# Masks of the maxima on GpSimd, maxima paced by an estimate, and an earlier start of the output weights in a hybrid S5 and attention step

## The chip, the cores and the metric

The kernel runs on one core of a Trainium2 chip. The metric is the device time of one execution in microseconds (us). The core has five engines that work side by side, each through its own queue: TensorE (PE: matrix products; PEld is its loading of weights), VectorE (DVE), ScalarE (ACT), GpSimd (POOL) and SyncE (SP), which here issues the DMA transfers. TensorE writes to banks of PSUM, and the on-chip memory for everything else is SBUF.

## The reference

One layer of an encoder is computed for a prompt of 2048 rows and for 64 further rows (the decode rows) with a cache of 512 earlier ones:

```python
mod = silu(c) @ w_ada + b_ada;  shift, scale, gate = split(mod)
proj = (rmsnorm(x) * (1 + scale) + shift) @ w_in
u, z_s, q, k, v, z_a, f_logit = split(proj)
y_ssm = gelu(s5(u)); y_ssm = y_ssm * sigmoid(y_ssm @ w_glu + b_glu) * silu(z_s)
s = q @ k.T * scale + cum_q - cum_k         # cum: running sum of log-sigmoid(f_logit)
s = where(pos_k <= pos_q, s, -inf)
y_att = softmax(s) @ v * silu(z_a)
y = x + gate * (concat(y_ssm, y_att) @ w_out)
```

There are 8 heads of 64 channels. The change touches the attention, from the scores to the softmax, and the loading of `w_out`. The softmax needs, for each query and head, the maximum of its scores; here it is found ahead of the scores themselves, by a cruder product.

## The kernel before

The program runs in stages: the modulation, the projection with the S5 part beside it (to about 742 us of the profile), the GLU of the S5 branch (to about 808), the attention (to about 1236) and the output projection (to the end).

**Tiles, blocks, units.** The heads go in four pairs, and a pair's two heads share the 128 partitions. For each pair there are five attention tiles, in the order of `self.order`: the decode rows (`qt` 4), then the prompt's queries in four tiles of 512 (`qt` 0 to 3). They are numbered 0 to 19, so 0, 5, 10 and 15 are decode tiles, and 4, 9, 14 and 19 are the longest. A tile's keys come in blocks of 128: 5 for a decode tile (four of the cache and one of the new rows) and 4, 8, 12 or 16 for the others. Two blocks make a unit of the loop in `run` (L1535). A unit computes the scores of its two blocks (`scores`, L1433: four passes for each head, then the exponential on ScalarE into a buffer `p`, then an addition of `p` to a running sum `acc`, on VectorE or POOL by turns), multiplies the unit before by the values (`mix`, L1480) and transposes one thing that was loaded (`turn`, L1343). The additions of `p` for a diagonal block after the first are narrower than 512 queries and all on VectorE.

**Loads.** `load` (L1279) is called twice a unit. It takes the next of `todo`, a tile of 512 keys or of 512 queries, when there are buffers for it. With the keys it also loads their forget bias `cb`, [128, 2, 512] in float32 and spread over all partitions, and holds it as long as the keys are used. There are six buffers for `cb` and three more from the start of the attention (L1514).

**Maxima.** A maximum (`maxima`, L1370) is one call for 128 queries of two heads against up to 512 keys: two matmuls into a twin bank, then two VectorE instructions that add the bias and take the maximum (L1398). Where the keys are those of the queries' own tile (the diagonal), or the new decode rows, four more matmuls add a mask `m_qk` through the identity `idb` (L1392 to L1394). Their order is the list `mx`: for each query tile, by 128 queries `t` and then by key tile. At most two are made for each of the 16 steps of the GLU (`MXU`, L1428) and two for each unit, one behind each block's scores (L1540), as long as there are any. When a tile's last is done, its maxima are transposed into `sm` by `turn`, and its scores can begin. There are 168 in all; 68 have a mask.

**Banks and order.** Scores and maxima share the twin banks in turn: two beside the GLU, three in the attention. TensorE's instructions keep the order in which the program writes them; the other queues are put in order by the planner at the time of building, which takes what is ready by its own reckoning.

**Output weights.** `Out.weights` (L1709) is a generator. Each step loads one block of `w_out`, 128x512, into one of three staging buffers `ost`, and for a block loaded two steps before it rounds the high part on ScalarE (`ohb`, L319) and subtracts on POOL to get the low part (`olb`, L205). It goes on only where SBUF is free. `run` begins with it when nothing is left of keys, queries and maxima (L1555) and then takes two steps a unit.

Of the kernel before, what the change touches and what calls it, by code (L numbers as in the profile page):

```python
# [17 lines left out]
P = 128  # L18
# [3 lines left out]
DEC = 64  # L22
# [20 lines left out]
PVG = 2  # L43
MXU = 2

# [144 lines left out]
def Step(tc, a, o, ctx):  # L190
# [76 lines left out]
    idb = [identb, cst.tile([P, P], BF16, name="identw")]  # L267
    m_qk, m_kq = ([cst.tile([P, P], BF16, name="%s%d" % (x, i)) for i in range(2)] for x in ("m_qk", "m_kq"))
    rj = cst.tile([P, P], F32, name="rj")
# [16 lines left out]
    def masks():  # L286
        tmp = Region(nc, R_S5W)
        swap = tmp.tile([P, P], F32, name="swap")
        PL.memset(swap, 0.0)
        for base in (64, -64):  # L290
            PL.affine_select(out=swap, in_=swap, compare_op=ALU.not_equal, fill=1.0, base=base,
                             pattern=[[-1, P]], channel_multiplier=1)
        V.tensor_copy(idb[1], swap)
        for sign, m in ((1, m_qk), (-1, m_kq)):
            for base in (0, 64, -64):
                x = tmp.tile([P, P], F32, name="msk")
                V.memset(x, 0.0)
                PL.affine_select(out=x, in_=x, compare_op=ALU.is_ge, fill=NEG, base=sign * base,
                                 pattern=[[-sign, P]], channel_multiplier=sign)
                r = slice(0, 64) if base == 64 else slice(64, P) if base else slice(0, P)  # L300
                V.tensor_copy(m[int(base != 0)][r], x[r])

# [867 lines left out]
class Attn:  # L1170
# [5 lines left out]
    def __init__(self, e):  # L1176
# [11 lines left out]
        self.cur = self.seen = self.unit = self.st = 0  # L1188
# [4 lines left out]
        self.todo, self.loaded, self.mx, self.smq = [], [], [], []  # L1193
        self.kv, self.values, self.q, self.ready = {}, {}, {}, {}
# [57 lines left out]
    def idle(self, tag):  # L1252

        now = self.seen if tag[0] == "c" else self.cur
        return sorted((x for x in self.held[tag] if x[2] < now), key=lambda x: x[2])
# [23 lines left out]
    def load(self):  # L1279
# [6 lines left out]
        if what == "k":  # L1286
            new = kind == "n"
            if not (self.can("kw" if new else "ks", 2) and self.can("cw" if new else "cb", 1)):
                return
# [11 lines left out]
            cb = self.claim([P, 2, w], "cw" if new else "cb", last, F32)  # L1301
            nc.sync.dma_start(cb, e.cb_d[2 * hp:2 * hp + 2, t0 * P:t0 * P + w].partition_broadcast(P))
            hi, lo = (self.claim([P, w], "kw" if new else "ks", last) for _ in range(2))
            self.kv[hp, kind] = hi, lo, cb, self.kb[:, t0 * P:], nt, rows, kind
        else:
# [37 lines left out]
    def turn(self):  # L1343
# [11 lines left out]
        elif self.loaded and self.loaded[0][0] + 2 <= self.unit:  # L1355
            _, (what, i, _), x, nt, rows, hi, lo = self.loaded.pop(0)
            pt = self.f.tile([P, 512], F32, tag="tr", name="tr")
            for t in range(nt):
                e.PE.transpose(pt[:, t * P:t * P + rows], x[:rows, t], e.ident[:rows, :rows])
            w = (nt - 1) * P + rows  # L1360
            e.S.copy(hi[:, :w], pt[:, :w])
            e.V.tensor_tensor(lo[:, :w], pt[:, :w], hi[:, :w], op=ALU.subtract)
            if what == "q":
                hp, qt = self.order[i]
                np = len(self.kinds(qt))
                for t in range(nt):
                    for pi in range(np):
                        self.mx.append((self.unit, i, t, pi, t == nt - 1 and pi == np - 1))

    def maxima(self):  # L1370

        e = self.e
        V, PE = e.V, e.PE
        if not self.mx or self.mx[0][0] >= self.unit:
            return
        _, i, t, pi, last = self.mx[0]
        hp, qt = self.order[i]
        if last and any(self.order[x[1]][0] == hp for x in self.smq):
            return
        self.mx.pop(0)  # L1380
        kinds = self.kinds(qt)
        nt = 4 if qt < 4 else 1
        if t == pi == 0:
            self.pm = self.mem.tile([P, 4, 2, 4], F32, tag="pm", name="pm")
        qh = self.q[i][0]
        kh, kl, cb, kb, kt, rows, kind = self.kv[hp, kinds[pi]]
# [3 lines left out]
        ops = [(ps[:, h, :n], qh[64 * h:64 * h + 64, ts], kh[64 * h:64 * h + 64, :n]) for h in range(2)]  # L1390
# [4 lines left out]
        self.pairs(ops, True, True)  # L1395
        for h in range(2):
            b = self.mem.tile([P, 512], BF16, tag="pb", name="pb")
            V.tensor_tensor_reduce(b[:, :n], ps[:, h, :n], cb[:, h, :n], 1.0, NEG, ALU.add, ALU.max,  # L1398
                                   accum_out=self.pm[:, t, h, pi:pi + 1])
        if last:  # L1400
            for h in range(2):
# [3 lines left out]
            self.seen = i + 1  # L1405

# [6 lines left out]
    def step(self):  # L1413
        self.unit += 1
        self.load()
        self.load()

    def glu(self, glu):
# [6 lines left out]
        for b in range(glu.steps):  # L1425
            self.step()
            glu.mm(b)
            for _ in range(MXU):  # L1428
                self.maxima()
            glu.part(b + 2)  # L1430
            self.turn()

    def scores(self, tile, kd, t):  # L1433

        e = self.e
        V, PL = e.V, e.PL
        kh, kl, cb, kb, kt, rows, kind = self.kv[tile.hp, kd]
        diag = kind == tile.qt or kind == "n"
# [54 lines left out]
    def sums(self, tile):  # L1493
# [12 lines left out]
        e.nc.sync.dma_start(e.ma_d[P * tile.hp:P * tile.hp + P, :, 64 * tile.qt:64 * tile.qt + n // TC], tile.z)  # L1506

    def run(self, out):

        e = self.e  # L1510
        self.f = Banks(e.psum, 0)
        for tag, kb, n in (("p", 4, 6), ("acc", 4, 4), ("z", 2, 2), ("w", 2, 2)):
            self.mem.ring(tag, int(1024 * kb), n)
        self.hold("cb", 4, 3)  # L1514
        weights = out.weights()
        pend = done = None
        self.forced = 0
        self.vload(0)
        for i, (hp, qt) in enumerate(self.order):
# [10 lines left out]
            e.nc.sync.dma_start(z, e.z_d[512 + P * hp:640 + P * hp, :, 64 * qt:64 * qt + nz // TC])  # L1530
            blocks = [(kd, t) for kd in self.kinds(qt) for t in range(self.kv[hp, kd][4])]
            tile = SimpleNamespace(hp=hp, qt=qt, nq=nq, nz=nz, z=z, q=self.q[i] + (self.ready[i],), acc=[None, None],
                                   given=[False, False], n=0, nb=len(blocks), po=None, rest=[],
                                   end=i >= len(self.order) - 2, last=i == len(self.order) - 1)
            for u in range(0, len(blocks), PVG):  # L1535
                self.step()
                group = []
                for kd, t in blocks[u:u + PVG]:
# [28 lines left out]
        out.mem.add(self.spare("vt"))  # L1567
        self.cur = self.seen = len(self.order)
        out.mem.add(self.spare("cb", "ks", "qs", "sm"))
        out.mem.join()  # L1570
# [84 lines left out]
class Out:  # L1655
# [12 lines left out]
    def __init__(self, e):  # L1668
# [4 lines left out]
        self.d, self.raw = [], []  # L1673
        self.near = self.cast = False
        self.ops = {}

# [32 lines left out]
    def weights(self):  # L1709
# [212 lines left out]
    def run(self, weights):  # L1922
# [14 lines left out]

        self.fetch("t3", 3, [self.mem.at("late", x, [P, 512], F32R) for x in self.mem.rings["ost"][2][1:]])
        for i, n in ((0, 1), (1, 1), (0, 0), (1, 0)):
# [195 lines left out]
```

## Time and profile before

| | us |
|---|---|
| median of 3 runs | 1406.46 (1403.91 to 1409.44) |
| span of the profiled execution, first to last instruction | 1410.9 |
| GLU | 742 to 808 |
| attention, 20 tiles | 812 to 1236 |
| last maximum starts | 1174.9 |
| first and last loads of output weights | 1107.2, 1222.6 |
| first and last subtractions of output weights | 1185.0, 1227.3 |
| span after the attention | 1236 to 1410.9 |

The profile comes from one execution and lists every instruction with its start, length, engine, line, and the tiles it writes and reads ("out<-in"). `twin` are banks of scores and maxima, `pb` and `pm` what a maximum writes, `p` the exponentials, `bank` other PSUM banks, `ohb`/`olb` the output weights. "Waits" name the engine and line that ended an idle time. A busy time of TensorE counts its instructions from start to modelled end; what a step costs is read from the starts of consecutive instructions.

### The profile page before, as it was taken

How to read it: one execution, taken by the hardware profiler on the slowest of the kernel's cores; microseconds unless marked ns; L12 is line 12 of the kernel's file. 1: busy time of each engine (PE TensorE's matmuls, PEld its weight loads, DVE VectorE, ACT ScalarE, POOL GpSimd, SP SyncE). 2: the span in 40 equal slices, each digit the busy share in tenths (PEclk: the TensorE clock that was granted, in tenths of full speed). 3: DMA queues.
4: the chain of work that ended last, by engine and by line, in shares of the span. 5: the costliest groups of instructions: out<-in, count | busy, mean ns of one | idle time of the engine just before them, and what ended most of it. 6: DMA issues, size and time to landing. Idle time of an engine off the chain costs nothing.

```text
span 1410.9 us, 25901 instructions
## 1 busy us (share of the span) xinstructions
PE 1318.9 (93%) x9164; PEld 1036.0 (73%) x9164; DVE 972.3 (69%) x2404; ACT 655.9 (46%) x1710; POOL 519.8 (37%) x502
## 2 busy tenths in 40 slices
PE   5898999999999899999899899999999999798998
PEld 2787999998888889898688755555555555387887
DVE  3635896987786679764326968786787786355775
ACT  3645365567443575574214435544544545522221
POOL 1100254566443446352004113423323325733453
PEclk9998999999999999999999979999999999999999
DMA  9894422534556835446239644124122123495542
GB/s 340 312 335 95 106 77 91 155 121 120 154 147 211 255 116 180 135 125 190 78 101 283 187 116 139 26 72 141 35 68 62 40 51 78 143 320 187 179 158 81
DMA packets 249476, 204.92 MB, mean 145 GB/s; under 512 B 91296, under 2 KB 217340, under 8 KB 248322
## 3 DMA queue, kind: packets, MB, share of 16 engines
q1 hardware_dynamic: 249346, 203.27, 47.0%
q8 instruction: 72, 1.18, 0.4%
q14 instruction: 58, 0.48, 0.1%
HBM read 137.68 MB, written 65.53 MB: 144 GB/s over the span
## 4 chain that ended last, share of the span: by engine, by line
PE 65%; DVE 13%; DMA 7%; issue 5%; ACT 3%; POOL 3%; SPq 3%; DVEq 0%; ACTq 0%; POOLq 0%
PE low L154 28%; PE twin L154 13%; PE bank L154 12%; PE last L154 7%; PE glu L154 2%; DMA wst<-in_w_in_dram 2%; DVE pb L1398 2%; PE bank L157 2%; DVE wlo L323 1%; POOL olb L205 1%; DMA x<-in_x_prompt_dram 1%; SPq L415 1%; PE low L157 1%; DMA lt<-t 1%; POOL qss L329 1%
## 5 line engine op out<-in xcount | busy, mean ns | idle before, releaser
L154 PE MATMUL low<-whi,h 128*128 128x256 f32 (+1 forms) x1584 | 294.6, 285 | 5.1 <-DVE th L608 4.0
L154 PE MATMUL low<-h,whi 128*128 128x256 f32 (+2 forms) x1152 | 277.3, 332 | 2.2 <-DVE th L608 1.4
L154 PEld LDWEIGHTS low<-whi,h 128*128 128x128 f32 x1584 | 248.1, 190 | 6.5 <-DVE th L608 4.2
L1398 DVE CUSTOM_DVE_ANT_0 pb<-twin,cb 128x512 bf16<-128x512 f32 (+3 forms) x328 | 200.0, 610 | 59.6 <-PE twin L154 49.8
L154 PE MATMUL low<-wlo,h 128*128 128x256 f32 (+1 forms) x816 | 229.7, 284 | 6.5 <-DVE wlo L323 6.5
L154 PEld LDWEIGHTS low<-h,whi 128*128 128x128 f32 x1152 | 197.3, 193 | 22.8 <-DVE h L323 1.9
L354 ACT ACTIVATE p<-twin 128x1024 f32<-128x1024 f32 (+3 forms) x180 | 149.8, 840 | 121.0 <-PE twin L154 110.7
L154 PE MATMUL low<-h,wlo 128*128 128x256 f32 (+2 forms) x576 | 189.4, 329 | 0.8 <-DVE wlo L323 0.8
L154 PEld LDWEIGHTS low<-wlo,h 128*128 128x128 f32 x816 | 154.8, 190 | 9.2 <-DVE wlo L323 8.8
L154 PE MATMUL bank<-p,vt 128*64 128x512 f32 (+3 forms) x704 | 143.2, 529 | 0.0
L154 PE MATMUL twin<-qs,ks 64*128 64x512 f32 (+3 forms) x1056 | 134.1, 359 | 0.0
L154 PEld LDWEIGHTS low<-h,wlo 128*128 128x128 f32 x576 | 111.4, 193 | 10.6 <-DVE wlo L323 1.9
L323 DVE TENSOR_TENSOR wlo<-wst,whi 128x512 fp32r<-128x512 f32 (+1 forms) x96 | 73.1, 767 | 66.4 <-ACT whi L319 66.1
L1476 DVE TENSOR_TENSOR acc<-acc,p 128x1024 f32<-128x1024 f32 (+4 forms) x88 | 90.1, 1024 | 30.0 <-ACT p L354 27.7
L329 POOL TENSOR_TENSOR qss<-qss,mhalf 128x4 f32<-128x4 f32 (+1 forms) x68 | 78.3, 1153 | 86.5 <-DVE qss L328 84.8
L154 PEld LDWEIGHTS twin<-qs,ks 64*128 64x128 f32 x1056 | 94.6, 190 | 11.0
L154 PE MATMUL twin<-sm,kb 64*128 64x512 f32 (+3 forms) x360 | 77.5, 426 | 22.2 <-DVE pm L1398 14.4
L154 PEld LDWEIGHTS bank<-p,vt 128*64 128x64 f32 x704 | 45.3, 140 | 64.5 <-issue 55.8
L319 ACT CAST whi<-wst 128x512 fp32r<-128x512 f32 (+1 forms) x96 | 58.8, 619 | 70.2 <-PE low L154 41.0
L205 POOL TENSOR_TENSOR x<-x,ot 128x512 f32<-128x512 f32 (+1 forms) x34 | 52.3, 1540 | 84.3 <-DVE ot L1803 79.3
L154 PEld LDWEIGHTS twin<-sm,kb 64*128 64x128 f32 x360 | 34.3, 186 | 63.0 <-DVE pm L1398 33.7
L645 ACT ACTIVATE hsq<-ev 128x64 bf16<-128x64 f32 (+1 forms) x272 | 69.8, 257 | 8.6
(437 smaller groups left out, 2641.6 us busy)
## 6 DMA issues: line engine op xcount, KB each, us to landing
wst<-in_w_in_dram SPq DMA_DIRECT2D x48, 512.0 KB
x<-in_x_prompt_dram SPq DMA_DIRECT2D x32, 512.0 KB
h<-h SPq DMA_DIRECT2D x16, 1024.0 KB
wada<-in_w_ada_dram SPq DMA_DIRECT2D x12, 1024.0 KB
cb<-cb_d SPq DMA_DIRECT2D x20, 512.0 KB
out_dram<-ev SPq DMA_DIRECT2D x64, 128.0 KB
out_dram<-x SPq DMA_DIRECT2D x32, 256.0 KB
z_d<-th SPq DMA_DIRECT2D x24, 256.0 KB
```

What stands on the lines that cost most here:

```text
L154: return self.keep(self.pe.matmul(*a, **kw))
L157: return self.keep(self.pe.transpose(*a, **kw))
L205: PL.tensor_tensor(out, x, y, op=op)
L319: i = S.copy(hi, x)
L323: V.tensor_tensor(lo, x, hi, op=ALU.subtract)
L329: PL.tensor_tensor(out, out, bc(mhalf[:out.shape[0]], list(out.shape)), op=ALU.pow)
L354: i = S.activation(out, x, func, **kw)
L415: x = nc.sync.dma_start(w[:, 4 * k2:4 * k2 + 4], e.w_ada[512 * k2:512 * k2 + 512, n * 512:n * 512 + 512] .rearrange("(k p) c -> p k c", p=P))
L645: S.activation(sq[:r], tv[:, h], AF.Square, accum_out=ss[:r, h:h + 1])
L1398: V.tensor_tensor_reduce(b[:, :n], ps[:, h, :n], cb[:, h, :n], 1.0, NEG, ALU.add, ALU.max, accum_out=self.pm[:, t, h, pi:pi + 1])
L1476: (PL if j else V).tensor_tensor(y[:rows, :, c0:nq], x[:rows, :, c0:nq], p[:rows, :, :n], op=ALU.add)
```

## The change

- **Masks.** `m_qk` becomes a float32 tile. The four mask matmuls go. Instead POOL adds the mask to the bias in place (`hide`): when the bias of a diagonal job is loaded, to its last 128 columns; after the maximum of 128 queries `t`, to the 128 columns before those, for the next one. So a job goes from `t` = 3 to 0.
- **Jobs and reloads.** The maxima are grouped in 48 jobs, one for each query tile and key tile. Each job loads its own bias into one of four buffers (`biases`, called once a unit), which comes free when the job is done. Before, the biases were loaded with the keys.
- **Pace.** `MXU` goes. `pace` keeps `lag`, an estimate of how far VectorE's work runs behind TensorE's: a unit adds VectorE's additions and takes off TensorE's time, a maximum adds the difference of its two shares. It makes up to two maxima while `lag` is below 2.3, and more only up to what is needed for the next tile to be ready (`left`); a second call after `turn` may make one more. Both calls stand behind the scores of both blocks.
- **Additions.** Narrower diagonal blocks now go to POOL by turns, too, once its running sum exists.
- **Output weights.** They begin when no keys and queries are left to load, one step a unit, and two once the maxima are done. There are four staging buffers, and a block is split three steps after its load. Once all maxima are done the subtraction is VectorE's. The SBUF that is given to them (`give`) includes what the smaller number of bias buffers leaves unused.

```diff
-MXU = 2
+GLU_PE, GLU_DVE, LAG = 3.7, 1.9, 2.3
...
-        for tag, kb, n in (("kw", 0.25, 4), ("vn", 0.5, 2), ("cw", 0.5, 2), ("cb", 4, 6), ("qs", 2, 12), ("sm", 2, 6),
+        for tag, kb, n in (("kw", 0.25, 4), ("vn", 0.5, 2), ("cw", 0.5, 2), ("cb", 4, 4), ("qs", 2, 12), ("sm", 2, 6),
...
+    def biases(self):
+        e = self.e
+        while len(self.bias_at) < len(self.jobs):
+            j = len(self.bias_at)
+            i, pi = self.jobs[j]
+            hp, qt = self.order[i]
+            kind = self.kinds(qt)[pi]
+            new = kind == "n"
+            if not self.can("cw" if new else "cb", 1):
+                return
+            w = DEC if new else 4 * P
+            t0 = 20 if new else 16 if kind == "c" else 4 * kind
+            cb = self.bias_at[j] = self.claim([P, 2, w], "cw" if new else "cb", j, F32)
+            e.nc.sync.dma_start(cb, e.cb_d[2 * hp:2 * hp + 2, t0 * P:t0 * P + w].partition_broadcast(P))
+            if new or kind == qt:
+                self.hide(cb, w)
+
+    def hide(self, cb, end):
+        w = min(end, P)
+        c = cb[:, :, end - w:end]
+        self.e.padd(c, c, self.e.m_qk[:, :w].unsqueeze(1).to_broadcast([P, 2, w]))
+
+    def left(self, i):
+        n = 0
+        for k, pi in self.jobs[self.job:]:
+            if k > i:
+                break
+            n += 4 if self.order[k][1] < 4 else 1
+        return n - self.place
...
+        t = nt - 1 - self.place
...
-        if kind == qt or kind == "n":
-            w = min(n, rows)
-            ops += [(ps[:, h, n - w:n], e.idb[m][64 * h:64 * h + 64], e.m_qk[m][64 * h:64 * h + 64, :w])
-                    for m in range(2) for h in range(2)]
...
+        if kind == qt and t:
+            self.hide(cb, t * P)
+        self.place += 1
...
+    def pace(self, pe, dve, least=0, most=2):
+        self.lag = max(0.0, self.lag + dve - pe)
+        done = 0
+        while done < most and (done < least or self.lag < LAG):
+            n = self.maxima()
+            if not n:
+                break
+            done += 1
+            self.lag += 2 * n / 960 + 0.25 - n / 2400
+        return done
...
-            for _ in range(MXU):
-                self.maxima()
+            self.pace(GLU_PE, GLU_DVE)
...
-        j = i % 2 if whole and not late else 0
+        j = i % 2 if not late and (whole or (acc[1] is not None and not tile.given[1])) else 0
+        if not j:
+            self.busy += 2 * n / 960 + 0.1
...
+    def give(self, out):
+        if not self.given:
+            self.given.append(None)
+            out.mem.add(self.ring("kn"))
+            out.mem.add([(a / 1024, b / 1024) for a, b in self.mem.segs if b > a])
+            self.mem.segs = []
+        out.mem.add(self.spare("ks", "qs"))
+        if len(self.bias_at) == len(self.jobs):
+            out.mem.add(self.spare("cb"))
+        if self.job == len(self.jobs) and not self.smq:
+            out.mem.add(self.spare("sm"))
...
-        self.hold("cb", 4, 3)
...
+        out.idle = lambda: self.job == len(self.jobs)
...
                 for kd, t in blocks[u:u + PVG]:
                     group.append(self.scores(tile, kd, t))
-                    self.maxima()
+                pe = 0.4 + sum(8.3 * x[4] for x in group) / 2400
+                units = (len(blocks) - u + PVG - 1) // PVG
+                need = self.left(i + 1)
+                need = -(-need // max(1, units - 1)) if need > 0 else 0
+                need -= self.pace(pe, self.busy, need)
...
-                if not (self.todo or self.loaded or self.mx or self.smq):
-                    if not self.given:
-                        out.mem.add(self.ring("kn"))
-                    out.mem.add(self.spare("cb", "ks", "qs", "sm"))
-                    next(weights, None)
+                self.pace(0.0, 0.0, need, 1)
+                if not (self.todo or self.loaded):
+                    self.give(out)
                     next(weights, None)
+                    if self.job == len(self.jobs):
+                        next(weights, None)
...
-        yield from wait(5)
-        mem.ring("ost", 2048, 3)
+        yield from wait(6)
+        mem.ring("ost", 2048, 4)
...
-            e.split(st, h, l, keep=True)
+            e.split(st, h, l, el=e.V if self.idle() else None, keep=True)
...
-                if len(late) == 2:
+                if len(late) == 3:
                     part()
```

More of the change, by code (lines that the diff above doesn't have):

```diff
@@ L267, in Step @@
     idb = [identb, cst.tile([P, P], BF16, name="identw")]
-    m_qk, m_kq = ([cst.tile([P, P], BF16, name="%s%d" % (x, i)) for i in range(2)] for x in ("m_qk", "m_kq"))
+    m_qk = cst.tile([P, P], F32, name="m_qk")
+    m_kq = [cst.tile([P, P], BF16, name="m_kq%d" % i) for i in range(2)]
     rj = cst.tile([P, P], F32, name="rj")
@@ L293, in masks @@
         V.tensor_copy(idb[1], swap)
[L294 to L301, printed above, removed]
+        V.memset(m_qk, 0.0)
+        PL.affine_select(out=m_qk, in_=m_qk, compare_op=ALU.is_ge, fill=NEG, base=0, pattern=[[-1, P]],
+                         channel_multiplier=1)
+        for base in (0, 64, -64):
+            x = tmp.tile([P, P], F32, name="msk")
+            V.memset(x, 0.0)
+            PL.affine_select(out=x, in_=x, compare_op=ALU.is_ge, fill=NEG, base=-base, pattern=[[1, P]],
+                             channel_multiplier=-1)
+            r = slice(0, 64) if base == 64 else slice(64, P) if base else slice(0, P)
+            V.tensor_copy(m_kq[int(base != 0)][r], x[r])
     mhalf = cst.tile([P, 1], F32, name="mhalf")
@@ L1287, in load @@
             new = kind == "n"
-            if not (self.can("kw" if new else "ks", 2) and self.can("cw" if new else "cb", 1)):
+            if not self.can("kw" if new else "ks", 2):
                 return
@@ L1363, in turn @@
             if what == "q":
[L1364 to L1368, printed above, removed]
+                self.qat[i] = self.unit
+    def biases(self):
[14 more added lines that the diff above has]
+                self.hide(cb, w)
@@ L1376, in maxima @@
-        _, i, t, pi, last = self.mx[0]
+        V = e.V
+        if self.job == len(self.jobs):
+            return 0
+        i, pi = self.jobs[self.job]
         hp, qt = self.order[i]
-        if last and any(self.order[x[1]][0] == hp for x in self.smq):
-            return
-        self.mx.pop(0)
         kinds = self.kinds(qt)
         nt = 4 if qt < 4 else 1
-        if t == pi == 0:
+        last = self.place == nt - 1
+        end = last and pi == len(kinds) - 1
+        if self.qat.get(i, self.unit) >= self.unit or self.job not in self.bias_at:
+            return 0
@@ L1384, in maxima @@
+        if end and any(self.order[x[1]][0] == hp for x in self.smq):
+            return 0
+        t = nt - 1 - self.place
+        if self.place == pi == 0:
             self.pm = self.mem.tile([P, 4, 2, 4], F32, tag="pm", name="pm")
         qh = self.q[i][0]
-        kh, kl, cb, kb, kt, rows, kind = self.kv[hp, kinds[pi]]
+        kh, kl, kb, kt, rows, kind = self.kv[hp, kinds[pi]]
+        cb = self.bias_at[self.job]
         ts = slice(t * P, t * P + P)
@@ L1399, in maxima @@
                                    accum_out=self.pm[:, t, h, pi:pi + 1])
+        if kind == qt and t:
+            self.hide(cb, t * P)
+        self.place += 1
         if last:
+            self.place = 0
+            self.job += 1
+        if end:
             for h in range(2):
@@ L1436, in scores @@
         V, PL = e.V, e.PL
-        kh, kl, cb, kb, kt, rows, kind = self.kv[tile.hp, kd]
+        kh, kl, kb, kt, rows, kind = self.kv[tile.hp, kd]
         diag = kind == tile.qt or kind == "n"
@@ L1567, in run @@
         out.mem.add(self.spare("vt"))
-        self.cur = self.seen = len(self.order)
-        out.mem.add(self.spare("cb", "ks", "qs", "sm"))
+        self.cur = len(self.order)
+        self.give(out)
         out.mem.join()
@@ L1674, in __init__ @@
         self.near = self.cast = False
+        self.idle = lambda: False
         self.ops = {}
@@ L1936, in run @@
         self.decode(0)
-        self.fetch("t3", 3, [self.mem.at("late", x, [P, 512], F32R) for x in self.mem.rings["ost"][2][1:]])
+        self.fetch("t3", 3, [self.mem.at("late", x, [P, 512], F32R) for x in self.mem.rings["ost"][2][:2]])
         for i, n in ((0, 1), (1, 1), (0, 0), (1, 0)):
```

26 lines of the change are left out of this document (13 added, 13 removed).

## The prediction

> **What bounds the kernel now.** I read the page first, then the windows by stage (cut where a tile of the attention begins), then who TensorE waits for in the stretches that are not full.
>
> ```profile
> span 1410.9 us, 25901 instructions
> ...
> PE 1318.9 (93%) x9164; PEld 1036.0 (73%) x9164; DVE 972.3 (69%) x2404; ACT 655.9 (46%) x1710; POOL 519.8 (37%) x502
> ```
>
> TensorE is the bound overall. The edits touch 742 to 1236 us. The columns are window, length, then busy time (instructions) of PE, PEld, DVE, ACT, POOL, the granted clock, DMA share, GB/s:
>
> ```profile
> core 0: us, PE busy (x) PEld busy (x) DVE busy (x) ACT busy (x) POOL busy (x), PEclk, DMA share, GB/s
> 742.00:812.00 70.00, 63.37 (x527) 57.58 (x527) 56.43 (x131) 31.46 (x61) 20.84 (x17) 0.99 0.80 239
> 812.00:835.00 23.00, 20.32 (x156) 13.14 (x154) 16.39 (x48) 6.28 (x14) 1.80 (x3) 0.65 0.54 157
> 835.00:922.00 87.00, 86.94 (x679) 46.86 (x675) 67.07 (x181) 43.49 (x54) 31.31 (x15) 1.00 0.27 73
> 922.00:940.00 18.00, 16.32 (x178) 10.70 (x178) 16.66 (x48) 7.50 (x15) 5.46 (x5) 1.00 0.29 75
> ...
> 1025.00:1044.00 19.00, 15.80 (x169) 9.91 (x169) 17.52 (x49) 7.13 (x15) 5.48 (x5) 1.00 0.22 56
> ...
> 1131.00:1150.00 19.00, 15.68 (x174) 9.92 (x174) 17.27 (x50) 6.92 (x14) 5.59 (x5) 1.00 0.27 47
> ...
> 1192.00:1236.00 44.00, 36.65 (x230) 17.21 (x230) 19.34 (x17) 23.27 (x34) 32.10 (x18) 0.92 0.53 147
> 1236.00:1411.00 175.00, 166.77 (x724) 136.51 (x720) 112.60 (x139) 35.61 (x62) 73.07 (x49) 0.97 0.54 185
> ```
>
> Long tiles (835 to 922) are TensorE's: 86.94 of 87, VectorE 77% busy. The three short stretches, where a head pair ends and two small tiles of the next begin, are VectorE's: 16.66 of 18, 17.52 of 19, 17.27 of 19. The last tile (1192 to 1236) is neither's: TensorE 36.65 of 44, POOL 32.10. TensorE's weight loads for the score banks wait there for the maxima (us, times, longest), in 811:835 and then the three short stretches:
>
> ```profile
> PEld twin L154 <- DVE pm L1398: 7.2, 4, 3.5
> ...
> PEld twin L154 <- DVE pm L1398: 3.1, 5, 1.2
> ...
> PEld twin L154 <- DVE pm L1398: 5.0, 7, 1.7
> ...
> PEld twin L154 <- DVE pm L1398: 5.1, 6, 1.5
> ```
>
> In the last tile it is a chain: a block of output weights waits for a free staging buffer, which POOL's subtraction gives back; ScalarE's rounding of that block waits for its landing; the exponentials stand behind the rounding.
>
> ```profile
> PE twin L154 <- ACT p L354: 7.3, 4, 2.3
> ...
> ACT ohb L319 <- DMA ost<-in_w_out_dram: 17.4, 7, 4.7
> ...
> SPq L1736 <- POOL olb L205: 22.6, 11, 4.2
> ...
> 1202.01 0.62 ACT L319 CAST ohb<-ost 128x512 fp32r<-128x512 f32 x1 [3.60 <-DMA ost<-in_w_out_dram]
> 1202.53 1.93 ACT L354 ACTIVATE p<-twin 128x1024 f32<-128x1024 f32 x2
> ...
> 1203.60 0.69 PE L154 MATMUL twin<-sm,kb 64*128 64x512 f32 x2 [2.33 <-ACT p L354]
> ```
>
> **The change, part by part.** Prices, mean ns behind the comma (the POOL rows with slashes give min/median/max):
>
> ```profile
> L1398 DVE CUSTOM_DVE_ANT_0 pb<-twin,cb 128x512 bf16<-128x512 f32 x232 | 159.5, 687 | 33.4 <-PE twin L154 27.0 <-DVE pm L1398 0.5 <-PE bank L154 0.3
> L1398 DVE DVE_READ_ACCUMULATOR2_ANT pm<- 128x1 f32 x336 | 27.8, 83 | 0.0
> ...
> L1476 DVE TENSOR_TENSOR acc<-acc,p 128x768 f32<-128x768 f32 x16 | 16.1, 1008 | 0.2
> ...
> L1362 DVE TENSOR_TENSOR ks<-bank,ks 128x512 fp32r<-128x512 f32 x20 | 13.8, 688 | 5.5 <-ACT ks L1361 5.5
> ...
> L1476 POOL TENSOR_TENSOR acc<-acc,p 128x1024 f32<-128x1024 f32 x22 | 52.3, 2379 | 44.1 <-ACT p L354 44.1
> ...
> L1476 POOL TENSOR_TENSOR acc<-p,p 128x256 f32<-128x256 f32 x4 | 2.9, 730 | 36.9 <-issue 26.4 <-ACT p L354 10.5
> ...
> L205 POOL TENSOR_TENSOR olb<-ost,ohb x16: 1264/1862/2264, 1185.0 to 1227.3; 128x512 fp32r<-128x512 f32 x16
> ```
>
> A full maximum (two heads, 512 keys) costs VectorE 2 x (0.687 + 0.083) = 1.54 us.
>
> *Output weights.* By the rules of the diff, counted unit by unit, the first block now starts in the last two units of tile 14 and ten of sixteen blocks are split, one a unit, before the last maximum; the other six go to VectorE (0.69 us each, the 688 row), which is busy 19.34 of 44 in the last tile. ScalarE's and POOL's shares move under tiles 14 to 18, where both have room (6.92 and 5.59 of 19): cost 0, or at most ten subtractions of 1.86 us = 19 us of POOL if its room is not where they fall. What goes is 7.3 us of TensorE's waits and, at clock 0.92, 0.08 x 44 = 3.5 us of slow clock. I take -10 of 10.8. Late next is TensorE itself. On SP the blocks now stand among the loads of values and gates of tiles 14 to 18, with one more staging buffer and a whole unit for each; one that waits there for POOL holds these loads up, which are a tile ahead: 0. The work after 1236 keeps its memory and its loads (the values' buffers still come free only then): 0.
>
> *Pacing.* Both versions make 20 maxima beside the GLU. Then tiles 0 and 1 get 4 instead of 9, and each of the three short stretches 5 instead of 9: 4 x 1.54 = 6.2 us less for VectorE in each, more than the 3.1, 5.0 and 5.1 us that TensorE waits. I take -11 of 13.2. In 811:835, of 7.2 us, 3.5 stand at the end of the GLU, where the last two maxima are as before or wider; the other 3.7 go: -4.
>
> ```profile
> 811.55 0.48 PE L154 MATMUL twin<-sm,kb 64*128 64x128 f32 x2 [3.22 <-DVE pm L1398]
> ...
> 810.00:815.00 5.00, 3.31 (x24) 2.73 (x25) 3.01 (x11) 0.98 (x3) 0.00 (x0) 0.62 1.07 291
> ...
> 820.00:825.00 5.00, 5.00 (x30) 3.08 (x30) 2.49 (x7) 0.97 (x2) 0.73 (x1) 0.51 0.70 207
> ```
>
> That stop is followed by half clock until 825, though TensorE is busy again from 811.55. [...]
>
> The removed maxima come back in the long tiles, up to three a unit: tiles 3 and 4 get 34 instead of 28. The estimate reckons 2 x 512/960 + 0.25 = 1.32 us for what the rows price at 1.54, and leaves out the key and query splits (0.69). For tiles 3 and 4 that is 6 x 1.54 = 9.2 us more on VectorE, less two diagonal pairs of adds (1.0 and about 0.5 us) that go to POOL: +6, where some 20 of 87 are idle, but in uneven lots. Its ends are 0, if the idle time takes it all, and three such pairs of tiles, 18; I take +5 over all of them, nearer the idle row.
>
> *Masks off TensorE.* Of 68 masked maxima, from the start of its score matmul to what follows:
>
> ```profile
> 1100.81 0.50 PE L154 MATMUL twin<-sm,kb 64*128 64x512 f32 x2
> ...
> 1101.84 0.40 PE L154 MATMUL twin<-ks,qs 64*128 64x512 f32 x2
> 1102.07 0.39 PE L154 MATMUL twin<-sm,kb 64*128 64x512 f32 x2
> ...
> 1108.39 0.50 PE L154 MATMUL twin<-ks,qs 64*128 64x512 f32 x2
> 1108.74 0.23 PE L154 MATMUL twin<-m_qk,identb 64*128 64x128 bf16 x2
> 1108.81 0.22 PE L154 MATMUL twin<-m_qk,identw 64*128 64x128 bf16 x2
> 1108.95 0.65 PE L154 MATMUL bank<-p,vt 128*64 128x512 f32 x2
> ```
>
> The masks take 1108.74 to 1108.95, 0.21 us. Some 40 of the 68 stand where TensorE is full: -8. Beside the GLU 14 of them save 3, and POOL's steps there (below) take 2: -1.
>
> *Masks onto POOL.* 64 additions of 128x256 at 0.73 and four half as wide: about 48 us on an engine with idle time everywhere. The price is a new wait. In a diagonal job the four maxima share one bias buffer: each must end before POOL masks 128 more columns, and the next cannot start before that. VectorE's adds are queued behind the waiting maximum, and TensorE waits for the bank it holds. Links between units have a whole unit (4 to 5 us); by my count 24 of 48 fall inside one. No row shows such a link. Its ends: 0, where the second maximum was late anyway, and 2.38 + 0.73 = 3.11, where a POOL add is just ahead. POOL is busy 31.31 of 87, so the likely delay is the mask and, 0.36 of the time, half an add: 0.73 + 0.36 x 1.19 = 1.16; VectorE's idle quarter and three score banks should hide more than half. I take 0.46 each: +11.
>
> On contention, the subtraction row goes from 1.26 to 2.26 us for one shape. [...] By that the masks would stretch by 1.86/1.26, to 1.08 us, an estimate from the row that belongs to the slow rival.
>
> *Bias reloads.* 48 loads instead of 24, 12 MB more, at a DMA share of 0.2 to 0.3 and four buffers deep (12 to 16 maxima ahead): 0; if one is late, POOL's mask stands at the head of POOL's queue with adds behind it, so up to some us, inside the range.
>
> Sum: -10 - 11 - 4 + 5 - 8 - 1 + 11 = -18 us. The profiled span of 1410.9 is 4.4 above the median of 1406.46; the differences are taken from the median: **1388.5**.
>
> **Rivals.** Gains alone are 34, the long tiles cost 5.
>
> *POOL's links decide (slower).* If POOL's queue puts its 2.38 us add ahead of the mask each time, a link delays 3.11 us, of which TensorE can cover one score block (1100.81 to 1101.84, 1.03): 2.08 x 24 = 50. That gives -34 + 5 + 50 = +21, 1427.5. It decides from (34 - 5)/24 = 1.2 us a link. For it: maximum, mask and add meet in the same unit. Against: POOL idle two thirds. 0.16.
>
> *VectorE's wait only moves.* The 15 us of the short stretches return in the long tiles: -10 - 8 - 1 + 11 + 5 = -3, 1403.5. For it: the estimate is low by 0.22 a maximum. Against: 77% busy there. 0.16.
>
> *The weights still come late* (POOL, fuller, gives the staging buffers back no sooner): -8, 1398.5. 0.05.
>
> [...] 0.16.
>
> **How the numbers follow.** Forecast 0.47 (its own range 1380 to 1398). About 0.5%, 7 us, is what a measurement of this kernel can tell from no change. Faster: 0.47 + 0.16 + 0.03 = 0.66; same 0.16 + 0.02 = 0.18; slower 0.16. The range reaches down to the everything-hidden case and up past the case of no change, 1369 to 1412; it leaves out the slow rival.
>
> **What would show it.** Right: short stretches with TensorE over 95% busy; no ScalarE wait for the weights' landing after 1150 and a last tile of some 34 us; long tiles as long as before. Wrong: VectorE's maxima idle for POOL by more than some 25 us in total, long tiles over 5 us a unit, or POOL waiting for bias loads.

## The result, and the profile after

| | before | after |
|---|---|---|
| median of the runs taken side by side, us | 1407.95 (1403.91 to 1410.27) | 1447.55 (1445.43 to 1450.98) |
| ratio, 95% interval | 1 | 1.0294 (1.0267 to 1.0321) |
| span of the profiled execution, us | 1410.9 | 1447.6 |

The kernel became 2.9% slower: 40 us, where 18 less were forecast. The page of after, its span and its engines:

```profile
span 1447.6 us, 25457 instructions
...
PE 1325.6 (92%) x8892; PEld 1035.7 (72%) x8892; DVE 966.7 (67%) x2385; ACT 651.2 (45%) x1710; POOL 594.0 (41%) x582
```

Little of this tells where the time went: TensorE has 272 products fewer (9164 - 8892) and yet 6.7 us more of busy time, VectorE is less busy, POOL 74 us more. The windows of after, in the columns of the prediction, on the long tiles 3 and 4, the three short stretches (tiles 5 and 6, 10 and 11, 15 and 16) and the last tile:

```profile
855.00:939.00 84.00, 73.10 (x481) 38.02 (x481) 58.53 (x163) 33.42 (x42) 44.23 (x31) 0.94 0.31 92
939.00:959.00 20.00, 16.71 (x161) 10.57 (x158) 11.73 (x34) 7.42 (x15) 7.82 (x8) 0.91 0.29 80
1054.00:1070.00 16.00, 13.92 (x155) 8.98 (x151) 11.90 (x36) 7.01 (x15) 8.65 (x9) 1.00 0.49 139
...
1174.00:1193.00 19.00, 15.71 (x148) 9.57 (x150) 11.49 (x32) 8.27 (x17) 12.56 (x11) 0.82 0.62 156
1241.00:1272.00 31.00, 31.00 (x222) 15.96 (x222) 14.68 (x16) 17.38 (x22) 11.47 (x5) 1.00 0.41 97
```

The last tile is full (31.00 of 31) where it was 36.65 of 44. The long tiles 3 and 4 took 68 us in before and were TensorE's throughout:

```profile
854.00:922.00 68.00, 67.94 (x527) 36.57 (x526) 53.39 (x146) 34.16 (x42) 27.28 (x13) 1.00 0.27 78
```

They now take 84, with 11 us of idle TensorE, and a clock of 0.94 where it was 1.00. VectorE has room there: 58.53 of 84. So neither engine is full. Who waits for whom, in the waits of after between 740 and 1280 us (total, times, longest):

```profile
PEld twin L154 <- DVE pm L1433: 70.9, 62, 5.0
PE twin L154 <- DVE pm L1433: 51.6, 54, 4.8
...
POOL cb L205 <- DVE pm L1433: 42.6, 26, 7.5
POOL cb L205 <- DMA cb<-cb_d: 38.3, 12, 7.4
DVE pb L1433 <- POOL cb L205: 34.4, 30, 5.7
```

TensorE waits for maxima, VectorE's maxima wait for POOL's masks, and POOL's masks wait for the maxima before them and for biases that have not landed. A link, below, is a maximum that waits in this way for a mask which POOL may add only when the maximum before it has ended. The second row stood so in before:

```profile
PE twin L154 <- DVE pm L1398: 15.6, 17, 3.2
```

One case of it, from the timeline of after in tile 13 (start, length, idle time before):

```profile
1115.98 0.72 POOL L205 TENSOR_TENSOR cb<-cb,m_qk 128x256 f32<-128x256 f32 x1 [7.36 <-DMA cb<-cb_d]
1116.67 2.34 POOL L1532 TENSOR_TENSOR acc<-acc,p 128x1024 f32<-128x1024 f32 x1
1118.96 0.73 POOL L205 TENSOR_TENSOR cb<-cb,m_qk 128x256 f32<-128x256 f32 x1
1119.72 0.56 DVE L1433 CUSTOM_DVE_ANT_0 pb<-twin,cb 128x384 bf16<-128x384 f32 x1 [5.71 <-POOL cb L205]
...
1120.95 0.45 PE L154 MATMUL twin<-ks,qs 64*128 64x256 f32 x2 [4.82 <-DVE pm L1433]
1121.32 3.52 PE L154 MATMUL bank<-p,vt 128*64 128x512 f32 x8
```

Read upwards from TensorE: it stood 4.82 us for a bank that a maximum held; VectorE stood 5.71 us with that maximum at the head of its queue for its mask, the third POOL row. The maximum before had ended at 1119.72 - 5.71 = 1114.01, so the mask could have run from then on; but in POOL's queue it stood behind an addition of 2.34 us, and that behind the first mask of a later job, which waited 7.36 us for its bias. Then the clock falls, in the windows of the same stretch:

```profile
1117.00:1121.00 4.00, 0.05 (x2) 0.05 (x2) 1.24 (x5) 0.01 (x1) 2.72 (x3) 1.00 0.00 0
1121.00:1124.50 3.50, 3.50 (x10) 0.90 (x10) 1.90 (x5) 0.00 (x0) 3.50 (x3) 0.52 0.00 0
```

The eight products of 1121.32 take 3.52 us at this clock. This wait so cost its own length and, by an estimate from this row, some 1.7 us (0.48 x 3.5) on top.

From the starts of the tiles' first score products, summed (us; "short" are tiles 0, 1, 5, 6, 10, 11, 15, 16, "second" 2, 7, 12, 17, "long" 3, 4, 8, 9, 13, 14, 18), with the runs that follow:

| kernel | short | second | long | last | attention |
|---|---|---|---|---|---|
| before | 79.0 | 74.7 | 226.8 | 43.6 | 424 |
| after | 72.2 | 80.0 | 272.3 | 31.7 | 456 |
| weights alone | 79.1 | 76.0 | 226.8 | 31.7 | 414 |
| masks back on TensorE | 64.9 | 78.3 | 239.7 | 31.7 | 414 |
| masks and pace back | 77.8 | 75.6 | 226.3 | 31.7 | 412 |
| first masks held | 73.2 | 79.0 | 260.5 | 31.7 | 445 |
| no links | 64.7 | 79.2 | 238.4 | 31.7 | 414 |
| links spaced | 66.2 | 77.6 | 250.0 | 31.7 | 425 |
| weights, fewer maxima in short tiles | 67.2 | 82.4 | 253.0 | 34.0 | 437 |

### The profile page after: what moved, and what is told of

It reads as the page before. It is cut to its first block, busy times and chain, and to the rows that moved or that the text cites. A ratio compares the mean times of both kernels' runs of the same rounds, so it can differ in the third digit from the quotient of the medians.

```text
span 1447.6 us, 25457 instructions
## 1 busy us (share of the span) xinstructions
PE 1325.6 (92%) x8892; PEld 1035.7 (72%) x8892; DVE 966.7 (67%) x2385; ACT 651.2 (45%) x1710; POOL 594.0 (41%) x582
## 3 DMA queue, kind: packets, MB, share of 16 engines
q8 instruction: 70, 1.15, 0.4%
## 5 line engine op out<-in xcount | busy, mean ns | idle before, releaser
L357 ACT ACTIVATE p<-twin 128x1024 f32<-128x1024 f32 (+3 forms) x180 | 146.2, 839 | 132.7 <-PE twin L154 128.9
L154 PE MATMUL bank<-p,vt 128*64 128x512 f32 (+3 forms) x704 | 149.0, 548 | 0.0
L1532 POOL TENSOR_TENSOR acc<-acc,p 128x1024 f32<-128x1024 f32 (+2 forms) x42 | 83.4, 1987 | 54.4 <-ACT p L357 54.2
L154 PE MATMUL twin<-ks,qs 64*128 64x512 f32 (+3 forms) x328 | 70.7, 451 | 30.2 <-DVE pm L1433 28.6
L1532 DVE TENSOR_TENSOR acc<-acc,p 128x1024 f32<-128x1024 f32 (+4 forms) x68 | 74.3, 1093 | 31.6 <-ACT p L357 30.7
L205 POOL TENSOR_TENSOR cb<-cb,m_qk 128x256 f32<-128x256 f32 x64 | 58.7, 917 | 88.5 <-DVE pm L1433 42.6
```

Of the source, the lines that this page charges most:

```text
L154: return self.keep(self.pe.matmul(*a, **kw))
L205: PL.tensor_tensor(out, x, y, op=op)
L357: i = S.activation(out, x, func, **kw)
L1532: (PL if j else V).tensor_tensor(y[:rows, :, c0:nq], x[:rows, :, c0:nq], p[:rows, :, :n], op=ALU.add)
```

## The experiments

The first four came together (before: 1408.13 us).

**The masks back on TensorE**, all else as after:

```diff
-            if new or kind == qt:
-                self.hide(cb, w)
...
-        if kind == qt and t:
-            self.hide(cb, t * P)
...
+        if kind == qt or kind == "n":
+            w = min(n, rows)
+            ops += [(ps[:, h, n - w:n], e.idb[m][64 * h:64 * h + 64], e.m_qk[m][64 * h:64 * h + 64, :w])
+                    for m in range(2) for h in range(2)]
```

> The changed kernel with its masks of the maxima back on TensorE as in the kernel before; pace, bias reloads, additions by turns and the early weights stay. POOL theory (VectorE's maxima wait for masks that stand in POOL's queue, 34.4 us in all, and TensorE for them): the long tiles come back to their old length, about 50 us less, about 8 us of mask matmuls more: 1395 us, 1385 to 1405. Pace theory (up to three maxima a unit are more than VectorE holds, wherever the masks are): at least 1425. Reload theory (the 44 bias loads stop SyncE's queue, and keys and queries come late): at least 1425.

Measured: 1401.97 us, ratio 0.9958 (0.9939 to 0.9977). The move of the masks alone costs 1447.55 - 1401.97 = 46 us; without it the change is a small gain.

**The early weights alone**, on the kernel before:

```diff
-                if not (self.todo or self.loaded or self.mx or self.smq):
...
+                if not (self.todo or self.loaded):
+                    self.give(out)
                     next(weights, None)
+                    if not self.mx:
+                        next(weights, None)
```

> The kernel before with the early start of the output weights alone (four staging buffers, one step a unit once no keys and queries are left, VectorE's subtraction once the maxima are done, memory as it comes free). The changed kernel's last tile was 11.9 us shorter. If that is the weights' doing: 1395 to 1399. If it hung on the other parts, too (on the memory of five bias buffers less): 1404 to 1408.

Measured: 1402.4, ratio 0.9962 (0.994 to 0.9984). Its last tile, in the windows:

```profile
1192.00:1224.00 32.00, 32.00 (x230) 16.58 (x230) 15.38 (x18) 17.37 (x22) 11.46 (x5) 1.00 0.37 91
```

It is full and 11.9 us shorter, and the other tiles stay. The timed runs give less, 5.4 us (2.3 to 8.4); the profiled executions differ by 12.5 (1410.9 to 1398.4). The profile of before is one of its longer executions; how much shorter its last tile is in the others, no run shows.

**The first mask of a job emitted later**, at the start of the job before (a method `first` that calls `hide`, in place of the call in `biases`):

```diff
+        self.first(self.job)
...
+        self.first(self.job + 1)
```

> The changed kernel, but the first mask of a diagonal job is not issued with the load of its bias: POOL adds it when the job before begins. The masks between the maxima of a job stay. If POOL's waits at the head of its queue for a bias that is still on its way (38.3 us, 12 times) are the larger share: some 20 to 30 us less, 1418 to 1428. If the masks between the maxima are: 1440 to 1448. Pace and reload theories: 1445 to 1450.

Measured: 1444.77, ratio 1.0275 (1.0236 to 1.0314). Its waits:

```profile
POOL cb L205 <- DMA cb<-cb_d: 37.9, 13, 7.5
DVE pb L1443 <- POOL cb L205: 37.5, 31, 5.8
```

POOL waits for landings as before the edit (38.3 us in 12 waits there): the later place in the program did not take these waits away. It says nothing on landings against links.

**The same with all masks on VectorE** (`e.V.tensor_tensor` in `hide`):

> As the run before this, with all 68 masks added by VectorE itself, so no maximum waits for another engine. A 128x256 addition there is 0.42 us at least by the additions of that width, 68 of them some 27 us more work for VectorE. POOL theory: 1395 to 1412. Pace theory (VectorE is too full already): slower than 1448, about 1460.

Measured: 1453.93, ratio 1.0327 (1.0301 to 1.0354). Its waits:

```profile
PE twin L154 <- DVE pm L1443: 57.2, 67, 3.8
DVE cb L1391 <- DMA cb<-cb_d: 30.7, 14, 3.8
```

Here a maximum and its mask are in one queue, and there is no link between engines. The time is that of the pace theory, and the expectation of the POOL theory failed, though the pace with the masks on TensorE had cost no such thing (1401.97). The masks in place are as dear on VectorE, now by its own time (68 additions more, some 27 us by the expectation's estimate of 0.42 us each) and by landings at the head of its queue (30.7 us in 14 waits). The two aren't told apart here.

The next four (before: 1409.24).

**The first masks held** back in POOL's queue, behind the first maximum of the job before; the links stay:

```diff
+        x = self.e.PL.tensor_tensor(c, c, self.e.m_qk[:, :w].unsqueeze(1).to_broadcast([P, 2, w]), op=ALU.add)
+        if after is not None:
+            self.e.tc.add_manual_dep(x.ins, after, self.e.nosync)
```

> The changed kernel (1447.55) with one thing altered: a job's first mask, the one that needs the bias to have landed, is held in POOL's queue until the last maximum of the job before; the other three masks of a job (the links) stay as they are. Theory 'landing' (the wait of POOL's queue for a bias that has not landed is most of the 46 us that the masks on POOL cost): POOL's waits for bias landings fall from 38 us to under 10, and the time to 1410 to 1425. Theory 'links' (each maximum of a diagonal job waits for a mask behind an addition on POOL): landings fall too, but VectorE still waits some 34 us for POOL's masks, and the time stays at 1437 to 1450.

Measured: 1432.42, ratio 1.0159 (1.0118 to 1.02): 15 of the 46 us, between the two expectations. (The expectation has the masks wait for the last maximum of the job before; the edit ties them to the maximum just made when `first` is called, which is the first one of that job, and only in the planner's order.) POOL's waits have no row for biases that had not landed any more, and the links are left:

```profile
PE twin L154 <- DVE pm L1445: 42.0, 55, 3.3
DVE pb L1445 <- POOL cb L1391: 24.7, 25, 2.9
```

**No links**: only a job's first mask is POOL's, the other three are products on TensorE:

```diff
-        if kind == qt and t:
-            self.hide(cb, t * P)
...
+        if kind == qt and t < 3:
+            w = min(n, rows)
+            ops += [(ps[:, h, n - w:n], e.idb[m][64 * h:64 * h + 64], e.m_qkb[m][64 * h:64 * h + 64, :w])
+                    for m in range(2) for h in range(2)]
```

> The changed kernel with one thing altered: only a job's first mask (and the decode rows' one) is added on POOL; the masks of its other three maxima are matmuls on TensorE as before the change, so no maximum waits for a mask between two maxima of its job. Theory 'links': the time falls by 30 us or more, to 1405 to 1418, with VectorE's waits for POOL's masks under 10 us. Theory 'landing': POOL still stands 30 us or more for biases at the head of its queue, and the time stays at 1430 to 1448. Both in equal parts: 1418 to 1430.

Measured: 1400.92, ratio 0.9946 (0.9922 to 0.997). All of the 46 us are gone, and more than the expectation of the links gave. VectorE's waits have no row for POOL's masks any more. Of the others:

```profile
POOL cb L205 <- DMA cb<-cb_d: 51.7, 13, 11.1
...
PE twin L154 <- DVE pm L1440: 23.8, 39, 3.3
```

POOL stands even longer for landings, 51.7 us, and it costs nothing against the masks on TensorE (1401.97). So in these runs a late bias was dear only where links stood behind it in POOL's queue.

**The masks and the pace back**, on the run with the masks on TensorE:

```diff
-            self.pace(GLU_PE, GLU_DVE)
+            self.maxima()
+            self.maxima()
...
                     group.append(self.scores(tile, kd, t))
+                    self.maxima()
...
-                need -= self.pace(pe, self.busy, need)
...
-                self.pace(0.0, 0.0, need, 1)
```

> The run with the masks back on TensorE (1401.97), with the pace undone too: two maxima a GLU step and one behind each block's scores, as before the change. Reloads of the biases, the order of the jobs, the additions by turns and the early weights stay. If the pace explains both the short stretches (-8) and the long tiles (+18): tiles 3, 4, 8, 9, 13, 14, 18 within 1 us of before, short stretches as before, and the time that of the early weights alone, 1402 (1399 to 1406). If the reloads or the additions by turns are what costs in the long tiles: these stay some 10 us or more longer, and the time is 1408 to 1418.

Measured: 1399.3, ratio 0.9924 (0.99 to 0.9949). The long tiles are those of before (226.3 and 226.8 in the table), and the short ones nearly so (77.8 and 79.0). So the pace is all of both differences, and the reloads of the biases and the additions by turns cost nothing that shows. Tiles 3 and 4 with the pace, in the windows of the run with the masks on TensorE:

```profile
846.00:919.00 73.00, 70.27 (x545) 38.29 (x545) 58.39 (x163) 33.37 (x42) 32.69 (x16) 1.00 0.35 105
```

and without it, in the run with the pace back:

```profile
851.00:919.00 68.00, 67.83 (x524) 36.48 (x521) 51.48 (x141) 34.17 (x42) 31.79 (x17) 1.00 0.34 98
```

VectorE's 6.9 us more came with maxima that were moved here. TensorE works 2.4 us longer, since they bring their products, and stands 2.6 us more (73 - 70.27 against 68 - 67.83).

**The early weights, and fewer maxima in the short tiles**, a simpler pace on the kernel before:

```diff
                     group.append(self.scores(tile, kd, t))
-                    self.maxima()
+                    if 0 < qt < 4 or len(group) == 2:
+                        self.maxima()
```

> The kernel before with the early weights, and with one maximum a unit instead of two in the decode tiles and the first query tile of each pair (none behind their odd block); in the longer tiles two a unit stay, and nothing else is changed. If VectorE's maxima bound the short stretches and the long tiles have room for as many as before at the same pace: the short stretches lose 2 to 3 us each and tiles 0 and 1 some 4, the long tiles stay, 1402 - 12 = 1390 (1386 to 1396). If the waits only move: 1400 to 1406. If the maxima come too late for the weights: the last tile is longer than 31.7 us.

Measured: 1421.89, ratio 1.0081 (1.0051 to 1.0111): 19 us slower than the weights alone, worse than any of the expectations. The short tiles lose 12 us, as was expected, but the second ones gain 6, the long ones 26 and the last one 2. Of the 26 us, 24 are in tiles 8, 13 and 18, each just ahead of the longest tile of its pair: by the order of TensorE's products these make 13, 15 and 14 maxima instead of 8, 11 and 3. The end of tile 8, in the windows:

```profile
976.00:980.00 4.00, 1.91 (x12) 1.17 (x10) 3.31 (x11) 1.00 (x2) 2.36 (x1) 0.85 0.69 229
980.00:985.00 5.00, 4.78 (x30) 3.56 (x32) 0.81 (x7) 1.75 (x3) 0.00 (x0) 0.50 0.45 166
```

and in the timeline:

```profile
977.25 0.29 DVE L1402 TENSOR_REDUCE mq<-pm 128x4 fp32r<-128x16 f32 x2
...
980.22 0.80 PE L154 MATMUL twin<-sm,kb 64*128 64x512 f32 x2 [0.67 <-ACT sm L1353]
```

The reduction of tile 9's last maxima starts at 977.25, and the first scores of that tile start at 980.22, behind their transposition and a copy. TensorE has little else to do (busy 1.91 of 4 us from 976 to 980), and then the clock is at 0.50. So the maxima in the short tiles bought a lead that the start of the longest tile needs.

The last two (before: 1408.49).

**The links spaced**: all 68 masks on POOL as in after, but the diagonal job taken by turns with the job before it, so that 36 of the 48 links have another maximum in between:

```diff
+        self.seq = []
+        for j, (i, pi) in enumerate(self.jobs):
+            qt = self.order[i][1]
+            if qt == 4:
+                self.seq.append((j, 0, 1))
+            elif pi == qt and qt:
+                self.seq += [(j - k, t, 2 * (t + k == 0)) for t in range(3, -1, -1) for k in (0, 1)]
...
+        job, t, step = self.seq[self.place]
...
+        self.job += step
```

> The changed kernel with all 68 masks still on POOL, but the diagonal job of a query tile taken by turns with the job before it, so that between two of its maxima stands one of the other job (not for the 12 links of the first query tile of each pair, which has no other job). Theory 'links' (what costs is that the next maximum waits for a mask that starts only when the one before it ends): VectorE's waits for POOL's masks fall from 34 us to under 12, and the time from 1447.55 to 1405 to 1425. Theory 'POOL's load' (48 more masks on POOL, by their time or by contention with VectorE, are what costs, and the run without links was fast because they were gone): it stays at 1435 to 1450.

Measured: 1412.0, ratio 1.0037 (1.0013 to 1.006): 36 of the 46 us. The masks' row on its page:

```profile
L205 POOL TENSOR_TENSOR cb<-cb,m_qk 128x256 f32<-128x256 f32 x64 | 58.7, 916 | 108.1 <-DVE pm L1439 56.5
```

is that of after's page:

```profile
L205 POOL TENSOR_TENSOR cb<-cb,m_qk 128x256 f32<-128x256 f32 x64 | 58.7, 917 | 88.5 <-DVE pm L1433 42.6
```

The load on POOL, 58.7 us, is the same, so it isn't what costs. What fell is the waiting on the other side, in its waits:

```profile
POOL cb L205 <- DMA cb<-cb_d: 50.9, 13, 10.3
PE twin L154 <- DVE pm L1439: 31.9, 35, 3.3
DVE pb L1439 <- POOL cb L205: 8.8, 8, 2.2
```

VectorE waits 8.8 us for masks instead of 34.4. Against after, the long tiles are 22 us shorter, the short ones 6 and the second ones 2. Against the run without links 11 us of attention remain, and they are in the long tiles (250.0 and 238.4; the others agree to 2 us). Whether they come from the 12 links that weren't spaced or from this order stays open.

**First masks on POOL, and the old pace**: the run without links, with the edit of the pace shown above:

> The run without links (a job's first mask and the decode rows' on POOL, the rest on TensorE, 1400.92) with the fixed pace of before: two maxima a GLU step and one behind each block's scores. If the pace of the change gives nothing net and TensorE's 20 masks fewer are a gain of their own: 1399 less 20 x 0.21 = 4, 1393 to 1399. If these masks were hidden anyway or the landings of biases now matter: 1399 to 1405.

Measured: 1399.82, ratio 0.9936 (0.9914 to 0.9958), the same as with all masks on TensorE (0.9924). Twenty masked products fewer give nothing that these runs can show. These two versions are the fastest found, some 9 to 10 us under the kernel before; that they beat the weights alone (1402.4) is within the intervals.

## Why the prediction was wrong

**Masks onto POOL: the step that failed.** "24 of 48 fall inside one ... VectorE's idle quarter and three score banks should hide more than half. I take 0.46 each: +11." The runs give 1447.55 - 1400.92 = 47 us by the medians, (1.0294 - 0.9946) x 1409 = 49 by the ratios: 1.94 us for each of the 24, not 0.46. The mechanism is the one that the prediction names, and so is the delay of a link ahead of any hiding: VectorE waited for masks 34.4 us in 30 waits, 1.15 in the mean, where the prediction had 1.16. The step that failed is that more than half of it would be hidden. The waits are uneven: in the timeline 21 of the 30 are 0.85 us or shorter, about a mask alone, and the longest, 5.7, lies beyond the upper end of 3.11. That 24 links matter wasn't tested by itself. Three things went into it wrongly:

- Idle time of VectorE hid little of the waits at the head of its queue. VectorE waited 34.4 us for masks, and TensorE's waits for maxima (`PE twin`) are 51.6 - 23.8 = 28 us longer than without links. VectorE was busy 77% in before, but what stood behind the waiting maximum couldn't run either, as in the timeline of tile 13.
- The price of a link was worked out from a mask and half an addition. In the trace the first mask of a *later* job stands before them and waits for its bias: 38.3 us in 12 waits. The prediction had named such a wait, with "up to some us, inside the range", and put the reloads at 0. By the run with the first masks held, it is 15 us: both terms were priced, but alone, and they cost when they meet in one queue.
- TensorE's stops were priced at their length. The windows of the attention, from some 8 us after its first scores on, of before:

```profile
820.00:1236.00 416.00, 396.72 (x3149) 217.20 (x3149) 308.66 (x773) 203.40 (x281) 163.19 (x86) 0.98 0.29 77
```

  of after:

```profile
824.00:1272.00 448.00, 401.28 (x2917) 214.96 (x2915) 303.48 (x768) 199.34 (x280) 230.30 (x156) 0.95 0.36 101
```

  and of the run without links:

```profile
820.00:1225.00 405.00, 387.33 (x3079) 213.44 (x3079) 298.90 (x766) 198.90 (x280) 193.32 (x114) 1.00 0.40 111
```

  By the clock, 0.05 x 448 = 22 us of after's attention are lost to half speed, 0.02 x 416 = 8 of before's, and next to nothing without links. Of the 47 us some 20 are this, by this estimate; the waits themselves, 28 us longer, are about the rest.

So the rival "POOL's links decide" was the case that came. Its price, 2.08 x 24 = 50, was right to 3 us, but partly by luck: it puts an addition of 2.38 us ahead of every mask, which most of the 30 waits are too short for, and it has neither the late biases nor the slow clock. Its time, 1427.5, was 20 short, because the gains that it kept were not there:

**Pacing: -11, -4 and +5 forecast, nothing or a small loss measured** (1401.97 with it and 1399.3 without; 1400.92 and 1399.82 without links). With the masks on TensorE the pace shortens the short tiles by 77.8 - 64.9 = 12.9 us, about what the two terms of -11 and -4 said. The second and long tiles get 318.0 - 301.9 = 16.1 longer, where +5 was taken ("nearer the idle row"; 18 was the other end). This is the rival "VectorE's wait only moves". The step left out that a maximum brings its products to tiles where TensorE was full, and put too much on idle time in uneven lots.

**Output weights: -10 forecast.** The tile is 11.9 us shorter, full at clock 1.00; 5.4 us of it (2.3 to 8.4) show in the timed runs. The mechanism is right: the other tiles pay 1.4 us in all, and TensorE is late next.

**Masks off TensorE: -8 and -1 forecast.** Not seen. Twenty of the 68 gave between a gain of 1.1 us and a loss of 0.5, against an expected gain of 4; the whole of it wasn't tried without links.

**On contention**, the stretch of the subtraction row gave an estimate of 1.08 us a mask. The row of the masks has 0.917 in the mean (median 0.736, longest 1.714), between that and 0.73: some of the masks stretch. What stretches them is not shown; the same mean, 0.916, costs little where the links are spaced (36 of the 46 us gone).

**The low end of the range**, 1369, took links at no cost and half clock after the GLU ending sooner than at 825. The links cost 1.94 us each, and the traces of before and after don't show such an early end: in before the clock stayed at 0.50 and 0.51 until 825, and in after, where TensorE began again at 816.24, it was 0.50 from 814 to 827.

Of the signs named beforehand, all three of the wrong ones came: VectorE idle for POOL 34.4 us (over 25), long tiles at (939 - 855)/14 = 6.0 us a unit (over 5), and POOL waiting for biases. Of the right ones only the last tile came (31.7 us, and no wait of ScalarE for a landing of weights after 1150).

## What to carry to other kernels

An addition that prepares the next step's operand *in place* made the steps a chain through two queues; price each link as mask plus whatever the other queue can put ahead of it, a late load included (0.73, 2.34 and 7.36 us in the timeline of tile 13), and hide none of it behind idle time of the engine that waits: 34.4 us of VectorE's waits came with 28 us more of TensorE's. The same masks on the same engine cost a quarter of it once another piece of work stood between most of the links (10 of 46 us were left). And work that was moved out of a stretch that waits brought all its engines' shares to where it went (12.9 us gained in the short tiles, 16.1 lost in the others), and, with the fewer maxima in the short tiles, took away the lead that it was building (24 us in tiles 8, 13 and 18).

## What was not expected of the hardware

A short stop cost twice. After a stop of 4.82 us TensorE ran 3.5 us at a clock of 0.52, though it was busy all the time; from 1124.5 to 1128 the clock was 0.99. It had been 1.00 ahead of the stop, from 1113 to 1117, so this wait cost more than its length, 1.7 us by the estimate above.

How long the clock stayed low did not go by the length of the stop. The 13 us of half clock at the end of the GLU, shown in the prediction, came after a stop of 3.22 us: TensorE was busy 5.00 of 5 us from 815 to 820, and again from 820 to 825, and the clock stayed at 0.50 and 0.51. In after a stop of 3.31 us, to 816.24, was followed by a clock of 0.50 until 827. What sets this time is not shown.
